# A triangular inverse done in place by columns, alpha folded into the residual addition, and new matmul prices for the list schedule

## Chip, cores and metric

The kernel runs on one core of one Trainium2 chip. The metric is device time in microseconds (us), median of several runs. The engines are named as the profile names them: PE (TensorE, matmuls; PEld is its weight loads), DVE (VectorE), ACT (ScalarE), POOL (GpSimd) and SP (SyncE, which issues the DMAs here).

## What is computed

Two transformer-like blocks of two layers each, for 256 tokens of 1024 features. The first block has modulated RMS norms, SwiGLU feed-forward parts, a differential attention with pooling, and a short convolution. The second block has deep-norm residuals, `layer_norm(alpha * h + branch)`, around a feed-forward part, a hybrid mixer and a second feed-forward part. The hybrid mixer holds a gated delta rule, for which a unit lower triangular system is solved per head and chunk. Cut to what matters here:

```
h = layer_norm(ALPHA * h + 0.5 * swiglu(h, ...), g1, b1)      # ALPHA = 4 ** 0.25, eps 1e-5
mix = hybrid_mixer(h, ...)                                    # delta rule + convolution (31 taps) + latent attention
h = layer_norm(ALPHA * h + mix, g2, b2)
h = layer_norm(ALPHA * h + 0.5 * swiglu(h, ...), g3, b3)
# inside the delta rule, per head and chunk:
a_mat = where(strict, beta * (k @ k.T) * decay, 0) + eye      # unit lower triangular
sol = triangular_solve(a_mat, rhs)
```

## The kernel before

Activations lie as [128 features, 256 tokens] tiles. Every large product is made of three fp32r matmuls (high times high, high times low, low times high): ACT casts a weight block to its high part (`whi<-raw`), DVE subtracts to get the low part (`wlo<-raw,whi`), and PE multiplies both with the two parts of the activations (`h`, `a`, `r`). In the trace these products write tiles named `mm`; small products in full fp32 write tiles named `sm`.

The program does not issue in the order in which it is written. The class `Order` takes down every instruction with what it reads and writes; `Order.price` gives each a cost in us, and `Order.schedule` makes a list schedule out of these prices, six rounds backward and forward. So a changed price or a changed dependency can move any instruction of any engine. Engines then run their queues strictly in that order.

The delta rule works on two chunks of 128 tokens per layer, four heads side by side, in `delta`. `products(tt)` makes the tile `NQ`: per head the system's matrix (transposed, only its strictly upper part counts) and the queries' part, which POOL masks with `tri_le`. `unit_inverse` inverts the four systems of a chunk by doubling blocks, in seven levels. At each level POOL masks the part of N that joins two blocks (`invN<-NQ,constt`, 128x512), PE multiplies it with the known inverse X, DVE adds the identity while it takes the result out of PSUM (`invW<-sm,constt`, 128x512), PE multiplies with Y, ACT copies the result out (`invX`), PE transposes it and ACT copies that (`invY`). `unit_inverse` is called four times in all (two layers, two chunks), and in each layer the two calls run interleaved, with the products of the delta rule's output gate (`mm<-whi,h` and `mm<-wlo,h`, 128x512) and of the mixer's other parts between them. In the same stretch DVE runs the 31 taps of the convolution (`cv<-gluu,colt,cv`, 240 instructions in two layers).

Deep norm: the tile x[m] holds alpha times h. `normed_begin.done` adds each chunk of a branch, and `end` normalises, cuts x into high and low parts and then lets POOL multiply x by ALPHA for the next residual (`x<-x`, `tensor_scalar`). `plain_begin` does the same at the entry of the second block.

Of the kernel before, what the change touches and what calls it, by code (L numbers as in the profile page):

```python
# [33 lines left out]
def _constants():  # L34
    """constants that depend on the shapes alone, as columns of one [128, n] array"""
# [9 lines left out]
    out.append(("cnt", np.tile(np.concatenate(cnt)[None, :], (P, 1))))  # L45
    for b in range(7):
        w = 1 << b
        out.append((f"level{b}", -1.0 * ((r // (2 * w) == c // (2 * w)) & (c // w % 2 == 1) & (r // w % 2 == 0))))
# [18 lines left out]
class Feat:  # L67
    """The activations a product reads: `norm`, pairs of (high, low) parts per 128 features. `early`: products
    that were already made, of what comes before the scale per token; `fix` mends them."""
# [5 lines left out]
class Spot:  # L75
    """a tile that gets its place when the instructions are put in order"""
# [16 lines left out]
class View:  # L93
    """a part of a Spot, with the offsets of its elements and the steps that lead to it"""
# [65 lines left out]
def lag(a, b):  # L160
    """from the end of an instruction of engine a to the start of one of b that reads what it wrote"""
    if a == b and a in ("PE", "DMA"):
        return 0.0
    return HOP[a] + (START if b == "DMA" else 0.0)


class Op:
    """instructions of one engine that follow each other"""
# [11 lines left out]
class Order:  # L180
    """Takes down the instructions of the whole computation with what they read and write, and issues them in the
    order of a list schedule: an engine that is free takes, of the instructions whose operands are there, the
    one that has to be over first if the whole is to end in time."""
# [19 lines left out]
    @contextmanager  # L203
    def in_turn(self):
        """the loads of the block go in the order in which they are written down"""
        self.turn = True
        yield
        self.turn = None

    @contextmanager  # L210
    def together(self):
        """the instructions of the block stay next to each other"""
# [31 lines left out]
    def touch(self, op, v, write, keep=False):  # L244
# [4 lines left out]
        # no two engines use a bank of PSUM at the same time  # L249
# [15 lines left out]
    def price(engine, name, out, ins, args, kw):  # L265
        """microseconds that an engine is held"""
# [9 lines left out]
        if engine == "PE":  # L276
            if name == "transpose":
                return 0.109
            return max(0.107, w / 2400.0) + 0.002 if ins[0].dt == F32R else max(0.217, w / 600.0 + 0.004)
# [26 lines left out]
    def schedule(self, canon, back):  # L306
        """list schedule; `canon`, an order that needs no more places than there are, gives the priorities. With
        `back`, time runs from the end to the beginning."""
# [5 lines left out]
        soon = {e: [] for e in ("PE", "DVE", "ACT", "POOL", "DMA")}    # by the time they can start  # L314
        now = {e: [] for e in soon}                                    # by their rank
# [5 lines left out]
        # room[kind][n]: places that stay free at step n of `canon`, with what is held by then  # L321
# [78 lines left out]
class Net:  # L400
    def __init__(self, nc, ins, cols):
# [10 lines left out]
        self.levels = [take(f"level{i}") for i in range(7)]  # L412
# [5 lines left out]
    def kept(self, shape, name, dt=F32):  # L418
        """a tile for the whole run"""
# [12 lines left out]
    def t(self, shape, name, dt=F32):  # L432
        """a short-lived tile"""
# [7 lines left out]
    def slot(self, name, dt=F32, width=T):  # L441
        """a tile of 128 features x 256 tokens that stays"""
        return self.nc.spot("big", [P, width], dt, name)

    def halves(self, name, n, width=T):
        """n pairs of tiles (high, low part)"""
        return [tuple(self.slot(f"{name}{i}{j}", F32R, width) for j in range(2)) for i in range(n)]

# [11 lines left out]
    def split(self, ap, n):  # L460
        """the (high, low) parts of the n pieces of a block of weights"""
# [8 lines left out]
        # at the start, before activations fill them, the small places serve too  # L470
# [24 lines left out]
    def linear_f(self, blocks, X):  # L495
        """blocks: DRAM APs [128, kc*M] that follow each other along the input features."""
# [1345 lines left out]
```

## Time and profile before

| | |
|---|---|
| median of 3 runs | 2349.83 us (2349.74 to 2353.2) |
| span of the profiled execution | 2349.6 us |
| PE busy | 2292.8 us, 98% |
| DVE busy | 1786.8 us, 76% |
| ACT busy | 1246.4 us, 53% |
| POOL busy | 143.4 us, 6% |

No time of its own is reported for the profiled execution; its span, from the first to the last instruction, is 0.2 us under the median. Busy PE time is modelled from the starts of pipelined matmuls, so a share of 98% says that PE is the engine to watch, not that its work could not be shorter. Where PE waits is read from short stretches.

### The profile page before, as it was taken

The numbers are of one execution on the slowest core, as the hardware profiler recorded it, in microseconds if no ns is written. First come the engines' busy times: TensorE is split into PE (matmuls) and PEld (weight loads), VectorE is DVE, ScalarE is ACT, GpSimd is POOL, SyncE is SP. The second block draws the span as 40 slices with busy tenths as digits, with TensorE's granted clock in tenths as the row PEclk, the third lists the DMA queues.
The fourth block names the chain that finished last, engine by engine and source line by source line (L and its number), as shares of the span: only waits on it lengthen the run. The fifth ranks groups of instructions, "written<-read, shape, count | busy, mean of one in ns | idle before, by whom it ended". The sixth has DMA issues, their size and how long they took to land.

```text
span 2349.6 us, 47411 instructions
## 1 busy us (share of the span) xinstructions
PE 2292.8 (98%) x18846; PEld 2260.3 (96%) x18846; DVE 1786.8 (76%) x3441; ACT 1246.4 (53%) x2129; POOL 143.4 (6%) x114
## 2 busy tenths in 40 slices
PE   5999999999999999999998999999999999999997
PEld 5999899999999999999998999999999989999997
DVE  7988998787778755665799959856856899769655
ACT  4445765455445544444573746644544655656543
POOL 0000100000000000100013000100100131002000
PEclk9999999999999999999999999999999999999998
DMA  8999478778777666765550445655565431555652
GB/s 312 340 318 324 130 272 293 269 268 293 266 254 240 186 186 189 236 187 179 167 169 17 151 140 192 207 181 183 184 186 176 147 124 49 173 163 195 196 180 84
DMA packets 139905, 470.30 MB, mean 200 GB/s; under 512 B 15777, under 2 KB 20897, under 8 KB 139682
## 3 DMA queue, kind: packets, MB, share of 16 engines
q1 hardware_dynamic: 139682, 467.27, 60.9%
q8 instruction: 148, 2.42, 0.4%
q14 instruction: 75, 0.61, 0.1%
HBM read 466.15 MB, written 1.05 MB: 199 GB/s over the span
## 4 chain that ended last, share of the span: by engine, by line
PE 83%; issue 8%; DVE 6%; DMA 2%; POOL 1%; ACT 0%; SPq 0%; POOLq 0%; DVEq 0%; ACTq 0%
PE mm L397 77%; PE sm L397 6%; DVE wlo L397 1%; DVE cv L397 1%; DMA raw<-in_w_ada_dram 1%; DVE x L397 1%; DMA raw<-in_ffn_wu_dram 0%; POOL x L397 0%; DVE raw L397 0%; DVE h L397 0%; DVE invW L397 0%; DVE invY L397 0%; DVE r L397 0%; DMA raw<-in_ffn_wg_dram 0%; DVE NQ L397 0%
## 5 line engine op out<-in xcount | busy, mean ns | idle before, releaser
L397 PE MATMUL mm<-h,whi 128*128 128x256 f32 x6848 | 1231.6, 282 | 11.2 <-DVE h L397 5.9
L397 ACT CAST whi<-raw 128x1024 fp32r<-128x1024 f32 (+5 forms) x811 | 786.1, 974 | 790.0 <-PE mm L397 381.6
L397 DVE TENSOR_TENSOR wlo<-raw,whi 128x1024 fp32r<-128x1024 f32 (+5 forms) x811 | 912.3, 1131 | 344.6 <-PE mm L397 281.4
L397 PEld LDWEIGHTS mm<-h,whi 128*128 128x128 f32 x6848 | 1054.3, 189 | 13.0 <-DVE h L397 7.5
L397 PE MATMUL mm<-h,wlo 128*128 128x256 f32 x3424 | 964.2, 282 | 0.2 <-DVE wlo L397 0.2
L397 PEld LDWEIGHTS mm<-h,wlo 128*128 128x128 f32 x3424 | 647.4, 189 | 0.4 <-DVE wlo L397 0.4
L397 PE MATMUL mm<-a,whi 128*128 128x256 f32 x2816 | 500.9, 281 | 0.0
L397 PEld LDWEIGHTS mm<-a,whi 128*128 128x128 f32 x2816 | 431.7, 188 | 0.1
L397 PE MATMUL mm<-a,wlo 128*128 128x256 f32 x1408 | 395.4, 281 | 0.0
L397 PEld LDWEIGHTS mm<-a,wlo 128*128 128x128 f32 x1408 | 265.1, 188 | 0.0
L397 DVE CUSTOM_DVE_ANT_0 raw<-raw,crep 128x1024 f32<-128x1024 f32 x144 | 175.5, 1221 | 67.6 <-DMA raw<-in_w_ada_dram 66.7
L397 PE MATMUL mm<-r,whi 128*128 128x258 f32 (+1 forms) x832 | 155.1, 287 | 0.0
L397 PEld LDWEIGHTS mm<-r,whi 128*128 128x128 f32 (+1 forms) x832 | 129.7, 190 | 0.0
L397 POOL TENSOR_TENSOR rstd<-var,constt 128x2 f32<-128x2 f32 x18 | 17.4, 966 | 1773.7 <-DVE var L397 1494.0
L397 PE MATMUL mm<-r,wlo 128*128 128x258 f32 (+1 forms) x416 | 118.8, 286 | 0.1
L397 DVE SCALAR_TENSOR_TENSOR cv<-gluu,colt,cv 128x256 f32<-128x256 f32 x240 | 116.9, 533 | 0.0
L397 ACT CAST a<-av 128x256 fp32r<-128x256 f32 x176 | 67.9, 404 | 40.2 <-DVE av L397 39.3
L397 ACT ACTIVATE sg<-mm 128x256 f32<-128x256 f32 x158 | 59.9, 380 | 55.2 <-PE mm L397 51.5
L397 DVE TENSOR_TENSOR a<-av,a 128x256 fp32r<-128x256 f32 x176 | 70.4, 421 | 24.7 <-ACT a L397 24.3
L397 PEld LDWEIGHTS mm<-r,wlo 128*128 128x128 f32 (+1 forms) x416 | 79.2, 190 | 0.4 <-DVE wlo L397 0.3
L397 POOL TENSOR_SCALAR x<-x 128x256 f32<-128x256 f32 x48 | 61.9, 1313 | 212.4 <-DVE h L397 212.4
L397 DVE TENSOR_TENSOR av<-mm,sg 128x256 f32<-128x256 f32 x158 | 65.9, 419 | 6.5 <-PE mm L397 5.5
(334 smaller groups left out, 2226.9 us busy)
## 6 DMA issues: line engine op xcount, KB each, us to landing
raw<-in_w_ada_dram SPq DMA_DIRECT2D x144, 512.0 KB, 4.9
raw<-in_ffn_wg_dram SPq DMA_DIRECT2D x88, 512.0 KB, 5.0
raw<-in_ffn_wu_dram SPq DMA_DIRECT2D x88, 512.0 KB, 4.7
raw<-in_ffn_wd_dram SPq DMA_DIRECT2D x64, 512.0 KB, 4.7
raw<-in_wi_gate_dram SPq DMA_DIRECT2D x48, 512.0 KB, 3.6
raw<-in_f1g_dram SPq DMA_DIRECT2D x44, 512.0 KB, 4.3
raw<-in_f1u_dram SPq DMA_DIRECT2D x44, 512.0 KB, 4.2
raw<-in_f2g_dram SPq DMA_DIRECT2D x44, 512.0 KB, 4.4
```

The costliest lines, as they stand in the source:

```text
L397: fn(*[real(a) for a in args], **{k: real(v) for k, v in kw.items()})
```

## The change

Three things change together.

1. `unit_inverse` works in place. POOL masks N once per call (`strict`), DVE adds the identity to it, and PE's first product of each level reads that whole matrix as its stationary operand, but only the columns of X that change at this level (64 of 128 per head). The part that joins two blocks is selected when DVE takes the product out of PSUM, by a multiplication with `level{b}` (128x256). The second product has 64 columns too. At the last level only a 64x64 quarter is made. ACT copies the changed columns back into X, with a stride.
2. ALPHA is no longer multiplied into x by POOL (48 `tensor_scalar` instructions). Since a layer norm does not see a common factor, x is kept as h, the residual is `ALPHA / scale * x + branch`, and eps is divided by scale squared. Chunks 0 to 3 get their factor where the branch is added, chunks 4 to 7 where the common shift is taken off.
3. `Order.price` has other prices for matmuls.

```diff
+    out.append(("strict", r < c))
     for b in range(7):
         w = 1 << b
-        out.append((f"level{b}", -1.0 * ((r // (2 * w) == c // (2 * w)) & (c // w % 2 == 1) & (r // w % 2 == 0))))
+        join = (r == c) - 1.0 * ((r // (2 * w) == c // (2 * w)) & (r // w % 2 == 1) & (c // w % 2 == 0))
+        if b == 0:
+            out += [("pair", join), ("pair_t", join.T)]
+        else:
+            out.append((f"level{b}", join[:, i // w % 2 == 0]))
...
-            return max(0.107, w / 2400.0) + 0.002 if ins[0].dt == F32R else max(0.217, w / 600.0 + 0.004)
+            return 0.0044 + w * 0.0004445 if ins[0].dt == F32R else max(0.224, w / 600.0 + 0.006)
...
         def done(m, ps):
-            nc.vector.scalar_tensor_tensor(out=x[m], in0=ps, scalar=scale, in1=x[m], op0=ALU.mult, op1=ALU.add)
+            if m < 4:
+                nc.vector.scalar_tensor_tensor(out=x[m], in0=x[m], scalar=ALPHA / scale, in1=ps, op0=ALU.mult, op1=ALU.add)
+            else:
+                nc.vector.tensor_tensor(out=x[m], in0=x[m], in1=ps, op=ALU.add)
...
-                for k in list(range(4, KD)) + list(range(4)):
+                for k in range(4, KD):
+                    nc.vector.scalar_tensor_tensor(out=x[k], in0=x[k], scalar=ALPHA / scale, in1=pb, op0=ALU.mult,
+                                                   op1=ALU.subtract)
+                for k in range(4):
                     nc.vector.tensor_tensor(out=x[k], in0=x[k], in1=pb, op=ALU.subtract)
...
                 self.cut(norm[m], x[m])
-                nc.gpsimd.tensor_scalar(out=x[m], in0=x[m], scalar1=ALPHA, scalar2=None, op0=ALU.mult)
...
-        nc.vector.scalar_tensor_tensor(out=var, in0=mm[:, 1], scalar=1e-5, in1=var, op0=ALU.add, op1=ALU.subtract)
+        nc.vector.scalar_tensor_tensor(out=var, in0=mm[:, 1], scalar=eps, in1=var, op0=ALU.add, op1=ALU.subtract)
...
     def unit_inverse(self, Nt):
         nc = self.nc
-        wide = [P, 4, P]
-        eye = self.ident.unsqueeze(1).to_broadcast(wide)
...
+        wide, H = [P, 4, P], P // 2
+        over = lambda m: m.unsqueeze(1).to_broadcast([P, 4, m.shape[1]])
+        nc.gpsimd.tensor_tensor(out=Nt, in0=Nt, in1=over(self.strict), op=ALU.mult)
+        nc.vector.tensor_tensor(out=Nt, in0=Nt, in1=over(self.ident), op=ALU.add)
...
-        for b in range(7):
-            # minus the part of N that joins two blocks
-            m = self.t(wide, "invN")
-            nc.gpsimd.tensor_tensor(out=m, in0=Nt, in1=self.levels[b].unsqueeze(1).to_broadcast(wide), op=ALU.mult)
-            ps = four(m, X) if b else turned(m)
-            w = self.t(wide, "invW")
-            nc.vector.tensor_tensor(out=w, in0=ps, in1=eye, op=ALU.add)
-            if b == 0:
-                X, Y = w, self.t(wide, "invY")
-                nc.vector.tensor_tensor(out=Y, in0=m, in1=eye, op=ALU.add)
-            elif b < 6:
-                X = kept(four(Y, w), "invX")
-                Y = kept(turned(X), "invY")
+        X, Y = self.t(wide, "invX"), self.t(wide, "invY")
+        nc.vector.tensor_tensor(out=X, in0=turned(Nt), in1=over(self.pair), op=ALU.mult)
+        nc.vector.tensor_tensor(out=Y, in0=Nt, in1=over(self.pair_t), op=ALU.mult)
+        for b in range(1, 7):
+            n = 1 << b
+            first = lambda h: X[:, h].rearrange("p (a t n) -> p a t n", t=2, n=n)[:, :, 0]
+            ps = self.psumx([P, 4, H])
+            for h in range(4):
+                nc.tensor.matmul(ps[:, h].rearrange("p (a n) -> p a n", n=n), Nt[:, h], first(h), start=True, stop=True)
+            w = self.t([P, 4, H], "invW")
+            nc.vector.tensor_tensor(out=w, in0=ps, in1=over(self.levels[b]), op=ALU.mult)
+            ps = self.psumx([P, 4, H])
+            if b < 6:
+                for h in range(4):
+                    nc.tensor.matmul(ps[:, h], Y[:, h], w[:, h], start=True, stop=True)
+                nc.scalar.copy(out=X.rearrange("p h (a t n) -> p h a t n", t=2, n=n)[:, :, :, 0],
+                               in_=ps.rearrange("p h (a n) -> p h a n", n=n))
+                ps, Y = turned(X), self.t(wide, "invY")
+                nc.scalar.copy(out=Y, in_=ps)
             else:
-                Y = kept(four(w, Y), "invY")
+                for h in range(4):
+                    nc.tensor.matmul(ps[0:H, h], w[:, h], Y[:, h, H:], start=True, stop=True)
+                nc.scalar.copy(out=Y[0:H, :, H:], in_=ps[0:H])
         return Y
```

What the schedule makes of it, at three places. First POOL's queue in the delta rule of the first hybrid layer, from the queries' and keys' norms (`rqk`) on. Before:

```order
L397 TENSOR_TENSOR rqk<-rqk,constt 128x16
L397 TENSOR_TENSOR invN<-NQ,constt 128x512 x12
L397 TENSOR_TENSOR rstd<-var,constt 128x2
L397 TENSOR_TENSOR invN<-NQ,constt 128x512 x2
L397 TENSOR_TENSOR NQ<-NQ,constt 128x512 x2
L397 TENSOR_TENSOR rstd<-var,constt 128x2
L397 TENSOR_TENSOR ro<-sso,constt 128x4 x2
```

Of the change, at the same place:

```order
L403 TENSOR_TENSOR rqk<-rqk,constt 128x16
L403 TENSOR_TENSOR NQ<-NQ,constt 128x512 x3
L403 TENSOR_TENSOR rstd<-var,constt 128x2
L403 TENSOR_TENSOR NQ<-NQ,constt 128x512
L403 TENSOR_TENSOR rstd<-var,constt 128x2
L403 TENSOR_TENSOR ro<-sso,constt 128x4 x2
```

Fourteen level masks and two `tri_le` masks of NQ became four 128x512 instructions: the strict mask and the `tri_le` mask of each chunk.

DVE's queue in the same stretch. Before, from the low part of a weight block (`wlo`) over the second chunk's first Y to two additions of the identity (`invW`), of which the second stands behind five taps of the convolution (`cv`):

```order
L397 TENSOR_TENSOR wlo<-raw,whi 128x1024
L397 TENSOR_TENSOR invY<-invN,constt 128x512
L397 TENSOR_TENSOR invW<-sm,constt 128x512
L397 TENSOR_TENSOR kfac<-rqk,eg 128x4
L397 TENSOR_SCALAR var<-sm 128x2
L397 SCALAR_TENSOR_TENSOR cv_15992<-gluu,colt,cv_15992 128x256
L397 SCALAR_TENSOR_TENSOR cv_16036<-gluu,colt,cv_16036 128x256
L397 SCALAR_TENSOR_TENSOR cv_15992<-gluu,colt,cv_15992 128x256
L397 SCALAR_TENSOR_TENSOR cv_16036<-gluu,colt,cv_16036 128x256
L397 SCALAR_TENSOR_TENSOR cv_15992<-gluu,colt,cv_15992 128x256
L397 TENSOR_TENSOR invW<-sm,constt 128x512
```

Of the change, at the entry of the first chunk's inverse: the addition of the identity to NQ (`NQ<-NQ,constt`), the first Y and the first X:

```order
L403 SCALAR_TENSOR_TENSOR NQ<-sm,rqk,decay 128x2x128
L403 SCALAR_TENSOR_TENSOR gluu<-glus,glua 128x256
L403 TENSOR_TENSOR sq<-sq 128x256
L403 SCALAR_TENSOR_TENSOR cv_15858<-gluu,colt,cv_15858 128x256
L403 TENSOR_TENSOR sq<-sq 128x256
L403 SCALAR_TENSOR_TENSOR NQ<-sm,rqk,decay 128x2x128
L403 TENSOR_TENSOR NQ<-NQ,constt 128x512
L403 SCALAR_TENSOR_TENSOR NQ<-sm,rqk,decay 128x2x128
L403 TENSOR_TENSOR invY<-NQ,constt 128x512
L403 SCALAR_TENSOR_TENSOR NQ<-sm,rqk,decay 128x2x128
L403 TENSOR_TENSOR invX<-sm,constt 128x512
L403 SCALAR_TENSOR_TENSOR NQ<-sm,rqk,decay 128x2x128
```

The wide additions of the identity out of PSUM gave way to one addition in SBUF ahead of the first transposes; `invY` and `invX` follow with one instruction of the other chunk between them.

Second, PE's queue in the same stretch. Before, from products of X with masked N to the products `invW,invY` and `invW,invN` of the two chunks:

```order
L397 MATMUL sm<-invX,invN 128x128 x3
L397 MATMUL sm<-constt,invX 128x128 x2
L397 MATMUL sm<-invX,invN 128x128
L397 MATMUL mm<-whi,h_15227 128x512
L397 MATMUL mm<-wlo,h_15227 128x512
L397 MATMUL mm<-whi,h_15277 128x512
L397 MATMUL mm<-whi,h_15239 128x512
L397 MATMUL mm<-wlo,h_15239 128x512
L397 MATMUL mm<-whi,h_15283 128x512
L397 MATMUL sm<-invW,invY 128x128 x4
L397 MATMUL sm<-invW,invN 128x128 x4
```

Of the change, from the transposes of the first chunk's N to the first product that reads X:

```order
L403 MATMUL sm<-constt,NQ 128x128 x4
L403 MATMUL mm<-h_15236,whi 128x256
L403 MATMUL mm<-h_15294,whi 128x256
L403 MATMUL mm<-h_15236,wlo 128x256
L403 MATMUL mm<-h_15296,whi 128x256
L403 MATMUL mm<-h_15317,whi 128x256
L403 MATMUL mm<-h_15296,wlo 128x256
L403 MATMUL mm<-h_15312,whi 128x256
L403 MATMUL mm<-h_15332,whi 128x256
L403 MATMUL mm<-h_15312,wlo 128x256
L403 MATMUL sm<-constt,sq 128x1 x2
L403 MATMUL sm<-invX,NQ 128x64 x4
```

The products of the first hybrid layer that stand between two steps of the inverse are other ones, and the new products have 64 columns (128x64).

Third, SP's queue near the start of the program, where the first modulation rows (`in_w_ada`) and the first weights are loaded. Before:

```order
L397 DMA raw<-in_w_ada_dram 128x1024 x2
L397 DMA raw<-in_ffn_wg_dram 128x1024
L397 DMA raw<-in_w_ada_dram 128x1024 x2
L397 DMA raw<-in_ffn_wu_dram 128x1024
L397 DMA raw<-in_w_ada_dram 128x1024 x2
L397 DMA raw<-in_ffn_wg_dram 128x1024
```

Of the change:

```order
L403 DMA raw<-in_w_ada_dram 128x1024 x2
L403 DMA raw<-in_ffn_wg_dram 128x1024
L403 DMA poolw<-in_pool_w_dram 128x256 x2
L403 DMA raw<-in_w_ada_dram 128x1024 x2
L403 DMA raw<-in_ffn_wu_dram 128x1024
L403 DMA raw<-in_w_ada_dram 128x1024 x2
```

The two loads of the pooling weights (`poolw`, read only by the attention part of the first layer) moved from there to the first loads.

## Rows read from the trace of the kernel before

**Rows 1.** Window: length, busy us (instructions) of PE PEld DVE ACT POOL, PEclk, DMA share, GB/s.

```profile
1200.00:1300.00 100.00, 93.52 (x732) 89.52 (x731) 94.94 (x215) 52.08 (x100) 25.48 (x19) 0.97 0.25 81
```

**Rows 2.** Short windows in the delta rule of both hybrid layers, same columns.

```profile
1240.00:1250.00 10.00, 9.21 (x81) 9.05 (x80) 9.39 (x17) 1.70 (x4) 5.62 (x4) 1.00 0.09 21
1250.00:1257.00 7.00, 6.56 (x51) 6.04 (x50) 7.00 (x8) 1.94 (x6) 5.78 (x5) 1.00 0.02 3
1257.00:1263.00 6.00, 1.55 (x7) 0.96 (x7) 6.00 (x11) 1.62 (x5) 3.61 (x3) 0.88 0.10 30
1263.00:1268.00 5.00, 5.00 (x20) 4.70 (x21) 3.83 (x9) 0.59 (x1) 2.98 (x3) 0.50 0.00 0
...
1917.00:1921.00 4.00, 0.66 (x6) 0.48 (x4) 4.00 (x6) 2.73 (x5) 4.00 (x4) 0.91 0.00 0
1921.00:1931.00 10.00, 9.73 (x73) 9.43 (x74) 10.00 (x22) 3.23 (x6) 2.93 (x3) 0.86 0.08 21
1936.00:1941.00 5.00, 1.28 (x11) 1.10 (x9) 5.00 (x8) 0.00 (x0) 2.67 (x3) 0.98 0.00 0
1941.00:1948.00 7.00, 6.72 (x45) 6.54 (x45) 6.15 (x10) 2.05 (x4) 4.18 (x3) 0.77 0.10 30
```

**Rows 3.** Timeline of PE: start, us, instruction, count, [idle before, releaser].

```profile
1262.83 2.05 PE L397 MATMUL sm<-invW,invY 128*128 128x128 f32 x8 [4.45 <-DVE invW L397]
...
1980.99 1.06 PE L397 MATMUL sm<-S,dn 128*128 128x128 f32 x8
```

**Rows 4.** Timeline of DVE in the same wait, same columns.

```profile
1258.35 3.74 DVE L397 SCALAR_TENSOR_TENSOR cv<-gluu,colt,cv 128x256 f32<-128x256 f32 x5
```

**Rows 5.** DVE's groups, 1244 to 1274: busy us, mean ns, idle before.

```profile
L397 DVE SCALAR_TENSOR_TENSOR cv<-gluu,colt,cv 128x256 f32<-128x256 f32 x24 | 16.7, 750 | 0.0
L397 DVE TENSOR_TENSOR invW<-sm,constt 128x512 f32<-128x512 f32 x6 | 4.1, 681 | 1.4 <-PE sm L397 1.4
L397 DVE TENSOR_TENSOR wlo<-raw,whi 128x1024 fp32r<-128x1024 f32 x2 | 3.3, 1662 | 0.0
L397 DVE TENSOR_TENSOR invY<-invN,constt 128x512 f32<-128x512 f32 x2 | 3.1, 1574 | 0.2 <-POOL invN L397 0.2
```

**Rows 6.** DVE's groups, 1280 to 1300, and a wide one of 1176 to 1184.

```profile
L397 DVE SCALAR_TENSOR_TENSOR cv<-gluu,colt,cv 128x256 f32<-128x256 f32 x27 | 11.8, 476 | 0.0
L397 DVE TENSOR_TENSOR invW<-sm,constt 128x512 f32<-128x512 f32 x5 | 3.4, 683 | 0.1
...
L397 DVE TENSOR_TENSOR wlo<-raw,whi 128x1024 fp32r<-128x1024 f32 x2 | 2.4, 1212 | 0.0
```

**Rows 7.** POOL's groups: of 1244 to 1274 the first two, of the span the third.

```profile
L397 POOL TENSOR_TENSOR invN<-NQ,constt 128x512 f32<-128x512 f32 x14 | 18.6, 1352 | 36.3 <-DVE NQ L397 29.7 <-PE sm L397 6.6
L397 POOL TENSOR_TENSOR NQ<-NQ,constt 128x512 f32<-128x512 f32 x2 | 2.5, 1270 | 0.0
...
L397 POOL TENSOR_SCALAR x<-x 128x256 f32<-128x256 f32 x48 | 61.9, 1313 | 212.4 <-DVE h L397 212.4
```

**Rows 8.** PE timeline of a one-column product; weight loads of 72 and 128 columns.

```profile
2335.11 0.58 PE L397 MATMUL sm<-constt,s 128*128 128x1 f32 x4 [1.07 <-DVE s L397]
2335.55 0.58 PE L397 MATMUL sm<-constt,sq 128*128 128x1 f32 x4
...
L397 PEld LDWEIGHTS mm<-r,whi 128*72 128x72 f32 x32 | 4.1, 142 | 0.0
...
L397 PEld LDWEIGHTS sm<-bv,invY 128*128 128x128 f32 x8 | 1.0, 192 | 0.0
```

**Rows 9.** A DVE group of the deep norms: ns min/median/max, first and last start.

```profile
L397 DVE TENSOR_TENSOR x<-x,lnw x48: 409/421/625, 1167.0 to 2345.8; 128x256 f32<-128x256 f32 x48
```

**Rows 10.** The start: its window, and the DMA issues of poolw (KB each, us).

```profile
0.00:52.00 52.00, 28.26 (x157) 24.40 (x157) 39.56 (x98) 21.40 (x40) 0.89 (x5) 0.97 0.86 304
...
poolw<-in_pool_w_dram SPq DMA_DIRECT2D x2, 128.0 KB, 4.4
```

**Rows 11.** Who waited, 640 to 692: us in total, times, longest.

```profile
PEld sm L397 <- DVE sq L397: 4.1, 1, 4.1
```

More of the change, by code (lines that the diff above doesn't have):

```diff
@@ L411, in __init__ @@
         self.neg_mask, self.mhalf, self.inv_cnt = take("neg"), take("mhalf"), take("cnt")
-        self.levels = [take(f"level{i}") for i in range(7)]
+        self.strict, self.pair, self.pair_t = take("strict"), take("pair"), take("pair_t")
+        self.levels = [None] + [take(f"level{i}") for i in range(1, 7)]
         self.swap, self.dup, self.dup_swap = take("swap"), take("dup"), take("dupswap")
@@ L1090, in end @@
             rn = self.t([P, 2, T], "rn")
-            nc.scalar.copy(out=rn, in_=self.spread2(*self.moments(st["s1"], st["s2"], D)))
+            nc.scalar.copy(out=rn, in_=self.spread2(*self.moments(st["s1"], st["s2"], D, 1e-5 / scale ** 2)))
             norm = [] if last else self.halves("h", KD)
@@ L1115, in normed_begin, with moments @@
         return done, end
-    def moments(self, s1, s2, n):
+    def moments(self, s1, s2, n, eps):
         nc = self.nc
@@ L1139, in take @@
             self.cut(pairs[m], xm)
-            self.nc.gpsimd.tensor_scalar(out=x[m], in0=xm, scalar1=ALPHA, scalar2=None, op0=ALU.mult)
         return take, lambda x, first: Feat(pairs)
@@ L1405, in unit_inverse @@
         nc = self.nc
-        wide = [P, 4, P]
-        eye = self.ident.unsqueeze(1).to_broadcast(wide)
-        X = Y = None
-        def four(lhs, rhs):
-            ps = self.psumx(wide)
-            for h in range(4):
-                nc.tensor.matmul(ps[:, h], lhs[:, h], rhs[:, h], start=True, stop=True)
-            return ps
-        def kept(ps, name):
-            o = self.t(wide, name)
-            nc.scalar.copy(out=o, in_=ps)
-            return o
+        wide, H = [P, 4, P], P // 2
+        over = lambda m: m.unsqueeze(1).to_broadcast([P, 4, m.shape[1]])
+        nc.gpsimd.tensor_tensor(out=Nt, in0=Nt, in1=over(self.strict), op=ALU.mult)
+        nc.vector.tensor_tensor(out=Nt, in0=Nt, in1=over(self.ident), op=ALU.add)
         def turned(a):
```

## The prediction

> **What bounds the kernel now.** I read the windows first, then the timelines of PE and DVE in the longest hole, then DVE's groups with and without POOL beside them. In the 100 us from 1200, where the first inverse runs, PE is busy 93.52 us, DVE 94.94 and POOL 25.48 [rows 1]: PE, which sets the end elsewhere, has holes there, and DVE is as full as PE. The short windows show where the holes are and what they cost [rows 2]. The idle PE time is 0.79 us (1240 to 1250), 0.44 (1250 to 1257) and 4.45 (1257 to 1263); in the second hybrid layer 3.34 (1917 to 1921), 0.27 (1921 to 1931), 3.72 (1936 to 1941) and 0.28 (1941 to 1948). That is 13.3 us. The reader should also look at the clock behind a hole: after the 4.45 us the granted clock is 0.50, that is 1.2 instead of 2.4 GHz, through the whole window 1263 to 1268, although PE is busy in all 5 us; eight fp32 matmuls take 2.05 us there against 1.06 us at full clock [rows 3]. A window of length L at mean clock c loses (1 - c) L: 2.5 us there, 1.4 in 1921 to 1931 (0.86) and 1.6 in 1941 to 1948 (0.77). So the inverse's holes cost 13.3 + 5.5 = **18.8 us**, 8.2 in the first hybrid layer and 10.6 in the second.
>
> Who makes the holes? The longest ends with DVE's `invW` [rows 3], and in front of it DVE ran five taps of the convolution in 3.74 us, 0.75 us each [rows 4]. Now compare DVE with itself. From 1244 to 1274, where POOL masks, a tap takes 750 ns, a wide `wlo` 1662, `invY` 1574 [rows 5]. From 1280 on, with POOL nearly still, a tap takes 476; a `wlo` outside takes 1212 [rows 6]. Yet `invW`, which reads PSUM and only one operand from SBUF, takes 681 and 683. So DVE instructions with two SBUF operands are slowed while POOL works. The excess is 24 x 0.274 + 2 x 0.45 + 2 x 0.89 (`invY` against the equally wide `invW`) = 9.3 us in the first layer, beside 14 + 2 wide POOL masks [rows 7]: 0.58 us of DVE delay for each mask, and the sum is about what PE loses there (8.2). Queues are strict, so a late tap makes `invW` late, and PE's next product.
>
> **The change part by part.**
>
> *POOL masks.* The order shows that 16 wide POOL instructions per layer become 4. At 0.58 us each, DVE is delayed by 2.3 us per layer instead of 9.3. If PE's loss keeps its proportion to the masks, a quarter of 18.8 stays, 4.7, and **14.1 us** go. Bounds: 0, if the taps in front of `invW` are what counts, whatever their speed; and 18.8, if DVE's slack now covers all. I take the proportion, since excess and loss agree so well.
>
> The Trainium skill (SBUF — State Buffer, "Who interferes with whom") says that a DVE instruction with two SBUF inputs contends with a GpSimd instruction that reads SBUF, and that the loser blocks for the whole instruction. The trace agrees on who is slowed. By a full block of 1.27 us for each of 4 masks, 5.1 of the 9.3 us of delay would stay per layer, 10.3 of the 18.8 us with them, and the time would come out near 2340 us instead.
>
> *DVE's own part of the inverse.* Per call seven `invW` and one `invY` become two SBUF instructions of that width, one X and six of half that width from PSUM. Eight whole widths become six, a gain of DVE time of at most 2 x 0.68 = 1.4 us per call, but for PE only slack. I count 0 beyond the proportion above.
>
> *PE's work.* Products and transposes are as many as before, but 128x64. What does half the columns save? A product with one column [rows 8] comes every 0.44 / 4 = 0.11 us (start 2335.11 to 2335.55, four records), the same as a record with 128 columns (eight in 1.06 us, less the last one's tail, 0.11 [rows 3]). So the weight load of 128 columns sets the pace, and 44 of a call's 48 fp32 products save nothing. Only the four last products have a stationary operand of 64 columns. A load of 72 columns takes 142 ns against 192 for 128 [rows 8], 0.89 ns per column: 64 fewer save 57 ns on each of 8 records, 0.46 us per call, **1.8 us** for four calls. Bounds 0 and 1.8; I take 1.8. Nothing hides it, PE being full around it; if PE waits there, it is worth 0.
>
> *The entry of a call* gets longer: strict mask, addition of the identity on DVE, transposes, then `invY` and `invX` before the first product. That is one DVE instruction more in front of the transposes, 0.68 us undisturbed and 1.57 with POOL beside it. What covers it: between the last product of a chunk and the transposes of its N the order of the first layer has 30 instructions of PE (18 of weights, 12 fp32 products of two records each), at 0.11 us or more a record over 4.6 us; between the transposes and the first product that reads X stand nine `mm` and two `sq` products (four records), some 1.5 us, for `invX` with one `invY` and two `NQ` in front. This cover is thin by up to a microsecond; I count it in the 4.7 that stays.
>
> *Alpha.* POOL loses 48 multiplications, 61.9 us of its time [rows 7], which nobody waits for: x is read again only when the next branch ends. Their price is again on DVE, where `x<-x,lnw` goes from 421 to 625 ns at most [rows 9], and the norms' ends have a few short PE waits. I take **1 us**, bounds 0 and 2. On DVE the instructions are exchanged one for one and cost the same.
>
> *The start.* The order moves two loads of 128 KB in front of modulation rows [rows 10]. The core loads at 304 GB/s there, and PE is busy only 28.26 of 52 us because it waits for data. 256 KB at 304 GB/s are **0.9 us later**; bound 0, if it falls where PE has work.
>
> *New prices* change ties all over the program. PE has no holes in the long feed-forward parts, so nothing is to gain there; the one other hole is 4.1 us before 690, where DVE is late behind a `w_ada` load [rows 11]. The order around it looks the same. I count 0, with 4 us either way.
>
> Sum against the span of 2349.6: -14.1 - 1.8 - 1.0 + 0.9 = -16.0, so 2333.6, and 0.2 more for the median of the runs shown: **2334 us**.
>
> **Rivals.**
>
> *All holes close.* Both the 18.8 and the 4.1 before 690 go: 2349.8 - 18.8 - 1.8 - 2 + 0.9 - 4.1 = 2324. For it: DVE gets about 7 us per layer back. Against: DVE stays above 90% full there [rows 1].
>
> *The holes stay.* The scheduler fills DVE with taps up to what it thinks PE needs, so `invW` again arrives just late, and only 1.8 us and 1 us less 0.9 remain: 2348, no measurable change (I call within 0.2%, 4.7 us, the same). For it: 27 taps fill DVE also from 1280 on [rows 6]. Against: there, undisturbed taps leave no hole.
>
> *Slower: the longer entry.* If at each of the four entries the identity and `invY` both run beside POOL's second mask (1.57 each [rows 5]) with a disturbed `wlo` (1.66) in front, PE comes 4.8 us late four times, 19.2 us, and each such hole costs half as much again at half clock (2.5 after 4.45 [rows 2]): 10.8. From 2334 that is 2364. It turns the sign when more than 3.9 us in all are lost per call, and reads as slower from some 5. Against it: the rows of PE between.
>
> *Columns count.* If a product's price followed its columns, 44 x 2 records in each of four calls would save 0.056 us: 19.7 us, 2314. The Trainium skill (TensorE: Matmul & The Clock Gate, "Back-to-back issue gap") has such a formula, N / 2.4 plus 2.5 ns, beside a warning that weight loads also set the spacing. The one-column rows speak against it.
>
> **How the numbers follow.** Chances: the forecast 0.60, all holes close 0.14, the holes stay 0.14, longer entry 0.06, columns 0.03, and 0.03 for a longer wait before 690 (2338). Faster by over 0.2%: 0.60 + 0.14 + 0.03 + 0.03 = 0.80; same 0.14; slower 0.06. The forecast's own range is 2326 to 2341 (a hole loss between 0 and 12). From 2322 to 2348 the range takes in the closing of all holes and most of the case that they stay; columns, the longer entry and a part of the same are left out.
>
> **What would show it.** POOL's busy time falls from 143 to below 60 us. Taps of the convolution stay near 476 ns between the masks. In the two stretches of the inverse PE's idle time is a few us in place of 13.3, and no window has a clock of 0.50. Records of products with 64 columns still start 0.11 us apart; the last level's start closer. A wait of PE for `invX` or the first `invW` would show the longer entry. The forecast fails if a hole that is no matter of POOL opens elsewhere, above all at the `w_ada` loads, or if the clock falls again behind one wait that is left.

## The result, and the profile after

The changed kernel takes 2368.43 us (median of 4 runs, 2364.04 to 2371.42); the kernel before, run beside it, 2349.78. The ratio is 1.0079 (95% interval 1.0066 to 1.0092): **slower by 18.7 us**, where a gain of 16 us was forecast. The profiled execution took 2366.18 us, its span is 2364.4. Its engines (busy us, share of the span, instructions):

```profile
PE 2302.6 (97%) x18846; PEld 2263.2 (96%) x18846; DVE 1756.5 (74%) x3445; ACT 1243.5 (53%) x2134; POOL 53.7 (2%) x42
```

POOL went from 143.4 to 53.7 us as forecast. But PE, with the same number of products, is busy longer and holds a smaller share of the span. The windows show where. First the two stretches of the inverse, which answer to [rows 1], and the start, which answers to [rows 10]:

```profile
1200.00:1300.00 100.00, 97.17 (x799) 93.94 (x797) 97.83 (x244) 61.89 (x129) 9.53 (x6) 1.00 0.35 111
1900.00:2000.00 100.00, 98.44 (x791) 94.91 (x792) 97.38 (x234) 54.36 (x105) 12.61 (x7) 0.98 0.29 95
0.00:52.00 52.00, 30.29 (x166) 25.91 (x166) 40.99 (x99) 20.72 (x39) 0.91 (x5) 1.00 0.89 309
```

and the second stretch before:

```profile
1900.00:2000.00 100.00, 92.38 (x715) 88.31 (x714) 97.81 (x209) 51.34 (x122) 26.15 (x20) 0.97 0.20 64
```

I count a window's loss as its idle PE time and (1 - clock) times its length. At 1200 and 1900 PE was busy 93.52 us [rows 1] and 92.38, both at clock 0.97: a loss of 6.5 + 7.6 + 3.0 + 3.0 = 20.1 us. Now it is 2.8 + 1.6 + 2.0 = 6.4. The changed kernel reaches its inverses later, at 1281 and 1956 us, and runs them past the ends of these windows; PE loses nothing from 1300 to 1360 and from 2000 to 2050. So the forecast's gain is there: 13.7 us. The loss lies in the first block, where none of the changed instructions stand. The changed kernel there:

```profile
150.00:175.00 25.00, 19.00 (x143) 17.79 (x142) 18.51 (x40) 9.35 (x15) 0.00 (x0) 0.91 0.80 272
175.00:200.00 25.00, 25.00 (x205) 25.00 (x204) 19.91 (x32) 10.15 (x13) 0.00 (x0) 0.95 0.92 318
225.00:250.00 25.00, 20.18 (x133) 18.75 (x133) 18.24 (x44) 13.07 (x19) 0.70 (x1) 0.80 0.73 249
500.00:525.00 25.00, 20.76 (x158) 19.31 (x156) 20.77 (x44) 11.15 (x17) 0.00 (x0) 0.94 0.81 256
525.00:550.00 25.00, 25.00 (x196) 25.00 (x196) 22.26 (x45) 12.33 (x20) 0.70 (x1) 0.92 0.70 233
700.00:725.00 25.00, 20.33 (x149) 19.55 (x149) 20.05 (x47) 13.43 (x19) 1.52 (x1) 0.86 0.82 287
```

and the kernel before at two of these places, and at its one hole, 675:

```profile
150.00:175.00 25.00, 25.00 (x214) 25.00 (x213) 20.98 (x40) 13.11 (x21) 0.00 (x0) 1.00 0.89 301
225.00:250.00 25.00, 25.00 (x151) 22.19 (x151) 22.38 (x56) 17.24 (x27) 2.67 (x3) 1.00 0.59 199
...
675.00:700.00 25.00, 21.11 (x156) 20.82 (x155) 18.58 (x48) 14.21 (x22) 1.54 (x1) 0.86 0.73 248
```

These six windows and the one from 300 to 350, with 1.4 us idle, lose 8.25 + 1.25 + 9.8 + 1.4 + 5.75 + 2.0 + 8.2 = 36.6 us, 15.5 of it by the clock (0.80 in 225 to 250). Before, only 675 to 700 loses: 3.9 idle + 3.5 by the clock, 7.4. The change's last window, 700 to 725, holds that same hole, come later by what was lost ahead of it: in both kernels PE waits there for DVE's `sq` (3.9 us before, 4.5 now). So the first block loses **29.2 us** more; less the 13.7 of the inverse and 3.6 of the first 52 us, 12 of the 14.8 us between the two spans are found, the rest in pieces of a us or two.

What does PE wait for there? The chain of work that ended last, in 50 to 260, with its shares by line; before:

```profile
by line: PE mm L397 97.9%; DMA raw<-in_ffn_wu_dram 2.5%; PE sm L397 1.1%; ACT whi L397 0.5%; DVE h L397 0.2%; ACT h L397 0.2%; issue 0.0%
```

and of the change:

```profile
by line: DMA raw<-in_w_ada_dram 36.9%; PE mm L403 30.4%; issue 11.2%; DVE wlo L403 10.2%; DMA raw<-in_ffn_wg_dram 3.6%; DVE raw L403 1.7%; ACT whi L403 1.2%; DVE r L403 1.2%; DVE adas L403 0.7%; DVE a L403 0.6%; PE sm L403 0.5%; DVE x L403 
```

Before, PE follows itself. Now loads of `w_ada` are more than a third of the chain. Who waited in 50 to 250 (us in total, times, longest), of the change:

```profile
DVE raw L403 <- DMA raw<-in_w_ada_dram: 29.6, 26, 3.0
...
SPq L403 <- DVE adas L403: 64.5, 34, 4.2
SPq L403 <- DVE wlo L403: 57.7, 50, 5.6
```

and before:

```profile
DVE raw L397 <- DMA raw<-in_w_ada_dram: 1.1, 1, 1.1
...
SPq L397 <- DVE wlo L397: 100.6, 62, 4.5
...
SPq L397 <- DVE adas L397: 17.3, 18, 2.0
```

`raw<-raw,crep` is DVE's reduction of a 512 KB piece of `w_ada`; its sum goes to `adas`. DVE now stands 26 times in front of a piece that has not landed, 29.6 us, against once. A piece, like a weight block, holds one of five `raw` places until DVE is through with it, and SP, whose queue is strict too, waits for a free place before it can issue a load. All its waits together are as long as before, 167.2 us against 166.3. What changed is who holds the place: it stands 64.5 us behind `w_ada` pieces (17.3 before) and 57.7 behind weight blocks that are still to be cut (100.6). So places that weights had are held by pieces that wait for DVE. I read it so that each late piece makes the next load late; the rows show the waits, not this order of cause and effect. From 100 to 150 the core loads at 298 GB/s, and before at 333, while PE, with weights cut ahead, is still full in both, first the change and then before:

```profile
100.00:150.00 50.00, 50.00 (x426) 50.00 (x425) 39.08 (x57) 21.93 (x33) 0.00 (x0) 1.00 0.87 298
```

```profile
100.00:150.00 50.00, 50.00 (x424) 50.00 (x423) 42.78 (x64) 24.05 (x34) 0.00 (x0) 1.00 0.93 333
```

From 156 us PE waits. DVE's timeline shows the first long hole made (start, us, instruction, [idle before, releaser]):

```profile
166.91 1.22 DVE L403 CUSTOM_DVE_ANT_0 raw<-raw,crep 128x1024 f32<-128x1024 f32 x1 [3.00 <-DMA raw<-in_w_ada_dram]
...
168.06 1.22 DVE L403 TENSOR_TENSOR wlo<-raw,whi 128x1024 fp32r<-128x1024 f32 x1
```

ACT's, at the same place:

```profile
168.57 0.83 ACT L403 CAST whi<-raw 128x768 fp32r<-128x768 f32 x1 [2.48 <-DMA raw<-in_ffn_wd_dram]
```

and PE's:

```profile
166.21 0.40 PE L403 MATMUL mm<-a,whi 128*128 128x256 f32 x2
...
169.76 0.84 PE L403 MATMUL mm<-a,whi 128*128 128x256 f32 x2 [3.03 <-ACT a L403]
```

DVE waits 3.00 us for a piece of `w_ada`, and a `wlo` stands behind it, which ends at 169.3. ACT waits 2.48 us for a weight block (`ffn_wd`), and behind it in ACT's queue stands the cast of `a` that PE needs, which starts at 169.3 too. PE idles 3.03 us, and its next two products take 0.84 us instead of 0.40; the granted clock is 0.66 from 170 to 180. Both strands begin with a load that comes late, and they end too close together to tell which of them held PE.

### The profile page after: what moved, and what is told of

Its sections match the earlier page's. It is cut to its first block, busy times and chain, and to the rows that moved or that the text cites. A ratio compares the mean times of both kernels' runs of the same rounds, so it can differ in the third digit from the quotient of the medians.

```text
span 2364.4 us, 47327 instructions
## 1 busy us (share of the span) xinstructions
PE 2302.6 (97%) x18846; PEld 2263.2 (96%) x18846; DVE 1756.5 (74%) x3445; ACT 1243.5 (53%) x2134; POOL 53.7 (2%) x42
## 4 chain that ended last, share of the span: by engine, by line
PE 80%; DVE 9%; DMA 7%; issue 2%; ACT 1%; POOL 0%; SPq 0%; DVEq 0%; POOLq 0%; ACTq 0%
PE mm L403 74%; PE sm L403 6%; DMA raw<-in_w_ada_dram 5%; DVE wlo L403 3%; DVE cv L403 1%; DVE raw L403 1%; DMA raw<-in_ffn_wg_dram 1%; DVE x L403 1%; DVE r L403 1%; DVE sq L403 0%; DVE h L403 0%; ACT whi L403 0%; DVE NQ L403 0%; DVE dnc L403 0%; DMA raw<-in_w_in_c_dram 0%
## 5 line engine op out<-in xcount | busy, mean ns | idle before, releaser
L403 PE MATMUL mm<-r,whi 128*128 128x258 f32 (+1 forms) x832 | 163.0, 294 | 9.2 <-ACT r L403 6.9
L403 DVE SCALAR_TENSOR_TENSOR cv<-gluu,colt,cv 128x256 f32<-128x256 f32 x240 | 106.4, 499 | 0.6
L403 ACT ACTIVATE sg<-mm 128x256 f32<-128x256 f32 x158 | 59.8, 378 | 29.2 <-PE mm L403 24.0
L403 PE MATMUL mm<-whi,h 128*128 128x512 f32 x160 | 58.5, 412 | 0.0
```

Of the source, the lines that this page charges most:

```text
L403: fn(*[real(a) for a in args], **{k: real(v) for k, v in kw.items()})
```

## Experiments

Times are medians; ratios are to the kernel before, run beside each. Its medians were 2349.35 (first four), 2348.35 (next four) and 2348.17 (last three).

**E1, old prices.**

```diff
-            return 0.0044 + w * 0.0004445 if ins[0].dt == F32R else max(0.224, w / 600.0 + 0.006)
+            return max(0.107, w / 2400.0) + 0.002 if ins[0].dt == F32R else max(0.217, w / 600.0 + 0.004)
```

> The changed kernel with the matmul prices of the kernel before, so only the inverse and alpha are changed. Theory P (the new prices reorder the first block so that DVE waits for w_ada loads, which cost PE some 31 us up to 725): the holes of 150 to 725 are gone and the time is about 2334 us, the forecast. Theory I (the inverse or alpha reorder the first block by themselves, for instance through the early poolw loads, and the prices are innocent): about 2366 us with the same holes. Theory L (the list schedule answers every small change with another order, some with holes and some without, and no part is to blame by itself): anything between, with holes at other places.

2331.45 us (four runs from 2327.22 to 2337.71), ratio 0.9933 (0.9911 to 0.9955). Theory P. The places of the holes are full:

```profile
150.00:175.00 25.00, 25.00 (x213) 25.00 (x213) 22.33 (x39) 13.28 (x21) 0.00 (x0) 1.00 0.91 331
225.00:250.00 25.00, 25.00 (x146) 21.98 (x146) 23.25 (x59) 16.32 (x26) 3.89 (x3) 1.00 0.56 178
1200.00:1300.00 100.00, 98.86 (x804) 95.08 (x804) 96.74 (x253) 58.28 (x138) 11.44 (x9) 1.00 0.28 86
1900.00:2000.00 100.00, 98.08 (x747) 90.06 (x746) 96.49 (x250) 63.38 (x160) 8.70 (x8) 1.00 0.26 81
```

The inverse's stretches lose 3.1 us here, 17.0 less than before.

**E2, new prices alone.** The kernel before with the `+` line of the change's price.

> The kernel before with only the new matmul prices. Theory P: slower by some 25 to 31 us, 2375 to 2381 us, with DVE waiting for w_ada loads between 150 and 725. Theory I: 2350 us, no change. Theory L: no fixed sign, some holes at places of its own.

2395.08 us, ratio 1.0198 (1.0183 to 1.0214): 45.7 us slower, the same holes in the first block (DVE's wait for `w_ada` in 50 to 250 is 30.4 us, 25 times). Theory P, some 14 us above its range. In windows of 10 us the stretch from 60 to 730 loses 39.2 us against 7.4 before, so the first block gives the 31 that were expected. The rest is spread over the second block: some 2 us in the old inverse, 5 from 1200 to 1220 and other small pieces.

**E3, the inverse alone**, and **E4, alpha alone**, each put into the kernel before with its old prices, by its part of the change's diff.

> The kernel before with only the inverse in place (old prices, alpha multiplied by POOL as before). Theory P: 2335 us, 14 to 16 us faster, and no holes in the first block. Theory I with the inverse to blame: about 2367 us. Theory L: the inverse's own gain of 14 to 18 us, read between 1200 and 2000, plus or minus holes elsewhere.

> The kernel before with only alpha folded into the residual addition (old prices, old inverse). Theory P: 2349 us, 1 us faster and nothing that a few rounds can tell from no change. Theory I with alpha to blame: some 2380 us with the holes of 150 to 725. Theory L: holes at places of its own, although alpha touches only the second block.

E3: 2333.35 us, ratio 0.9933 (0.9918 to 0.9947), 16.0 us faster. E4: 2348.07 us, ratio 0.9995 (0.9986 to 1.0004), not to be told from no change. Theory P in both. E4 shows one thing more. Up to 725 us every queue of it has the instructions of the kernel before in the same order, and yet its trace loses 2.9 us from 60 to 730, where the kernel before loses 7.4, all at the hole before 690. So the size of that hole in one trace is partly chance. In E1 and E3 the `poolw` loads stand where they stood before, at 216 and 217 us, so neither the inverse nor alpha moves them.

**Why do the prices do this?** While the first feed-forward runs, the program asks for 0.8 pieces of `w_ada` per weight block, that is for 1.8 loads; after the attention part of the first layer it asks for 0.5 (`ADA_RATES = 0.8, 0.0, 0.5`). A block feeds 24 products. So four more kernels each change how one of these, the product or the load, is priced.

**E5**, of the change:

```diff
-            return 0.0044 + w * 0.0004445 if ins[0].dt == F32R else max(0.224, w / 600.0 + 0.006)
+            return max(0.107, w / 2400.0) + 0.002 if ins[0].dt == F32R else max(0.224, w / 600.0 + 0.006)
```

> The changed kernel with the old price for fp32r products and the new one for fp32 products. In the first feed-forward of the first block 24 fp32r products and 1.8 loads belong together: with the old price the schedule reckons 24 x 0.109 = 2.62 us of PE against 1.8 x 1.454 = 2.62 us of loads, with the new one 24 x 0.1182 = 2.84 against 2.62. Theory R (the fp32r price alone tips that balance, so that loads and w_ada reductions no longer count as urgent, and the load stream falls behind): about 2331 us, as with all old prices. Theory F (the fp32 price matters too): clearly over 2340.

2331.52 us, ratio 0.9929 (0.9912 to 0.9945). The new fp32 price does no harm; the fp32r price is the one that does.

**E6, a longer latency of loads**, of the change with its new prices:

```diff
-HOP = {"PE": 0.31, "DVE": 0.13, "ACT": 0.14, "POOL": 0.1, "DMA": 1.0}
+HOP = {"PE": 0.31, "DVE": 0.13, "ACT": 0.14, "POOL": 0.1, "DMA": 2.05}
```

> The changed kernel, new matmul prices, with 2.05 instead of 1.0 us from the end of a load's price to its use, so that issue to use is 4.7 us in the schedule as in the trace (before it reckons 1.2 + 1.454 + 1.0 = 3.65). Theory D (what is too short in the schedule's eyes is the latency of a load: DVE's w_ada reductions are placed a microsecond before their data land): most of the 31 us come back, some 2335 to 2345. Theory R (the ratio of load price to PE price counts, not the latency): still holes in the first block, 2355 to 2370.

**E7, a dearer load**, of the change with its new prices:

```diff
-            return n(v) * v.shape[0] / 128 * 0.00142
+            return n(v) * v.shape[0] / 128 * 0.00154
```

> The changed kernel, new matmul prices, with the price of a load raised by 8.5% from 1.454 to 1.577 us per 512 KB (the rate the trace shows in that stretch, 334 GB/s, gives 1.57). 1.8 loads then cost 2.84 us in the schedule, as much as the 24 products. Theory R: the holes of the first block are gone, 2330 to 2338 us. Theory D: little changes, 2355 to 2370. Theory L (any new order is a draw): no fixed place.

E6: 2337.12 us, ratio 0.995 (0.9935 to 0.9966). E7: 2346.61 us, ratio 0.9988 (0.9978 to 0.9998). Each theory has a part, in a stretch of its own. The two traces come from runs of nearly the same time, 2342.65 us (the slowest of E6's four) and 2341.88 (the fastest of E7's ten). Windows of E6:

```profile
225.00:250.00 25.00, 18.83 (x104) 17.26 (x105) 20.01 (x44) 13.53 (x23) 0.70 (x1) 0.86 0.63 203
500.00:525.00 25.00, 23.27 (x193) 22.86 (x192) 22.80 (x43) 12.88 (x20) 1.61 (x1) 1.00 0.66 220
675.00:700.00 25.00, 24.40 (x205) 24.12 (x204) 21.03 (x48) 13.06 (x18) 0.70 (x1) 1.00 0.85 299
```

and of E7:

```profile
225.00:250.00 25.00, 24.72 (x144) 21.84 (x145) 21.75 (x53) 18.38 (x28) 3.13 (x3) 1.00 0.74 234
500.00:525.00 25.00, 21.75 (x162) 21.45 (x163) 22.17 (x41) 11.10 (x18) 0.69 (x1) 0.86 0.70 220
675.00:700.00 25.00, 20.44 (x161) 19.29 (x161) 20.54 (x44) 13.18 (x20) 0.00 (x0) 0.98 0.79 265
```

E7 leaves 0.3 us idle in 225 to 250, 1.9 in 200 to 225 and none in 150 to 175, where 1.8 loads stand beside 24 products, but keeps the holes at 500 and 675, where a block has 1.5 loads. E6 leaves 1.7 and 0.6 us idle there, and keeps 6.2 at 225. Theory R, which took the price for all, is too narrow.

**E8, the old ratio broken from the other side**: all old matmul prices, and `0.00131` in the line of E7.

> The changed kernel with all old matmul prices, and the price of a load lowered by 8% to 1.341 us per 512 KB: 1.8 loads cost 2.41 us against 2.62 of PE, the ratio of the changed kernel, although no matmul price is new. Theory R: the holes come back at the same places, some 2355 to 2370 us, with SP waiting for w_ada reductions between 50 and 150. Rival (the new matmul prices do it in another way, for instance through PE's own order): about 2331 us.

2360.58 us, ratio 1.0034 (1.0014 to 1.0053): 29 us slower than E1 by the medians (19 to 30 over its five runs), with the old matmul prices.

```profile
150.00:175.00 25.00, 21.97 (x172) 21.57 (x172) 19.69 (x40) 10.06 (x16) 0.00 (x0) 0.94 0.84 285
225.00:250.00 25.00, 20.65 (x142) 19.59 (x142) 20.61 (x50) 15.65 (x24) 0.70 (x1) 0.86 0.65 216
700.00:725.00 25.00, 21.09 (x152) 20.67 (x151) 22.44 (x58) 12.55 (x21) 1.54 (x1) 0.86 0.56 175
```

The holes of the changed kernel are back at its places (the one at 500 too, with 3.3 us idle), and Theory R's range is met. So a load priced too low against PE opens them without any new matmul price, and it is no draw of the order. The ratio is not all of it: E7, which restores it, keeps some of the holes, and E6, which leaves it as in the change, is rid of some.

**E9, both corrections of the load**, the edits of E6 and E7, with the new matmul prices.

> The changed kernel, new matmul prices, with both corrections of the loads together: 1.577 us per 512 KB and 2.05 us from its end to the use. The price alone cleared the first 175 us but left holes at 475 to 550 and 675 to 725, where a block has 1.5 loads and the schedule still sees slack; the latency alone cleared those and left some 9 us at 200 to 250. Theory RD (both are needed, each for its stretch, and the matmul prices are harmless once the loads are priced as truly): first block without holes, 2326 to 2333 us. Theory L (each order is a draw): 2335 to 2360, holes at new places.

2328.9 us, ratio 0.9919 (0.9902 to 0.9935). Its windows:

```profile
225.00:250.00 25.00, 24.36 (x150) 21.64 (x149) 22.53 (x51) 16.79 (x26) 3.56 (x2) 1.00 0.64 224
...
675.00:700.00 25.00, 25.00 (x213) 25.00 (x213) 22.73 (x57) 15.88 (x26) 1.54 (x1) 1.00 0.63 212
```

Theory RD. The new matmul prices do no harm once the loads are priced by what the trace shows. Side by side, with the loss from 60 to 730 (my sum over windows of 10 us) and the time that DVE waited for `w_ada`, all in us:

| kernel | fp32r price | load price | load latency | loss, 60 to 730 | waits, 50 to 250 | waits, 450 to 725 |
|---|---|---|---|---|---|---|
| before | old | old | old | 7.4 | 1.1 | 41.8 |
| E1 | old | old | old | 1.0 | 0.5 | 22.2 |
| the change | new | old | old | 36.4 | 29.6 | 54.2 |
| E7 | new | dearer | old | 19.5 | 5.3 | 50.2 |
| E6 | new | old | longer | 13.2 | 15.3 | 16.6 |
| E9 | new | dearer | longer | 1.6 | none | 11.8 |
| E8 | old | cheaper | old | 25.0 | 11.3 | 47.3 |

The waits of the first stretch go mostly with the price, those of the second with the latency. A wait of DVE alone does not make a hole: the kernel before has 41.8 us of it in the second stretch and loses 7.4.

**E10, POOL's masks given back**, on E1, in each level of the inverse:

```diff
+            idle = nc.gpsimd.tensor_tensor(out=self.t(wide, "invM"), in0=Nt, in1=over(self.strict), op=ALU.mult)
             w = self.t([P, 4, H], "invW")
...
+                op.before.add(idle)
```

> The changed kernel with old matmul prices (2331.45 us), and twelve 128x512 multiplications per hybrid layer given back to POOL in the inverse, whose results nobody reads: six per call, one a level, as before. DVE's, ACT's and PE's own work is that of the changed kernel. Theory C (the forecast's: POOL's masks slow DVE's two-operand instructions by 0.58 us each, and PE loses as much): 7 us per layer come back, some 2343 to 2347 us, with convolution taps at 700 ns and more in the inverse. Theory W (the holes closed because DVE's and PE's own work in the inverse got less or moved; POOL beside it hardly matters to PE): 2330 to 2335 us.

2352.56 us, ratio 1.0014 (1.0004 to 1.0024): 21.1 us more than E1 by the medians. Windows of E10:

```profile
1200.00:1300.00 100.00, 93.51 (x737) 88.75 (x736) 97.41 (x230) 51.47 (x111) 23.89 (x19) 0.97 0.22 66
1900.00:2000.00 100.00, 91.94 (x702) 86.60 (x701) 94.74 (x213) 48.66 (x122) 25.36 (x20) 0.93 0.19 60
```

DVE's taps of the convolution in 1235 to 1275 (busy us, mean ns), of E10:

```profile
L403 DVE SCALAR_TENSOR_TENSOR cv<-gluu,colt,cv 128x256 f32<-128x256 f32 x44 | 26.3, 648 | 0.0
```

and of E1:

```profile
L403 DVE SCALAR_TENSOR_TENSOR cv<-gluu,colt,cv 128x256 f32<-128x256 f32 x54 | 25.0, 510 | 0.0
```

Theory C, and more than it asked: 6.5 + 8.1 us idle and 3.0 + 7.0 by the clock, 24.6, against 3.1 in E1. DVE's, ACT's and PE's own work is the same, and no engine waits for one of the new masks in the trace, so what they cost comes of standing beside DVE, or of the order that they leave, which differs from E1's from 336 us on.

**E11, old matmul prices with E6's latency.**

> The changed kernel with old matmul prices and the truer latency of loads (2.05 us for 1.0). Its first block has no holes with old prices, so the latency can gain only 2 us around 690; 2326 to 2333 us if order elsewhere stays as good. Theory L: several us either way.

2326.46 us, ratio 0.9911 (0.9896 to 0.9926): the fastest here, 21.7 us under the kernel before. DVE's wait for `w_ada` in 450 to 725 falls from 22.2 us in E1 to 2.9. Its interval overlaps those of E1 and E9, so the last few us are not certain. It comes near the 2324 of the rival in which all holes close.

## Why the prediction was wrong

**The step that failed** is the one on the new prices: "PE has no holes in the long feed-forward parts, so nothing is to gain there ... I count 0, with 4 us either way." That there is nothing to gain does not mean that there is nothing to lose. Measured: 37.0 us by the medians (the change against E1), or 45.7 on the old inverse (E2). The full windows of PE were a balance. In 100 to 150 the kernel before makes 424 products, 24 in 2.83 us, and loads at 333 GB/s with the DMA engines 0.93 busy: 512 KB in 1.57 us, 1.8 of them in 2.83. PE and the loads are both nearly full. The old prices had both 8% too cheap (2.62 and 2.62), and so in balance. The new price corrected one side only: by its prices the schedule now has 8% of slack for the loads. That this opens the holes is shown (E1, E5, E8); that the schedule ranks loads and reductions as less urgent for it is my reading of the program, and no run shows the ranks. The prediction's last lines did name the place, a hole "above all at the `w_ada` loads", but as a thing to look for: it had 0.03 and 4 us, with no price worked out for a whole stretch that falls behind. The latency adds to it. The schedule reckons 1.2 + 1.454 + 1.0 = 3.65 us from issue to use; the page of the changed kernel (KB each, median us from issue to landing) says

```profile
raw<-in_w_ada_dram SPq DMA_DIRECT2D x144, 512.0 KB, 4.7
```

about a microsecond more; E6 and E9, which put it in, show that it matters. That the order "looks the same" around the `w_ada` hole was read off the sequence; how far ahead the loads run was not considered. That hole before 690 [rows 11] may be the same fault, already in the kernel before: E9's trace does not have it (25.00 busy in 675 to 700). But since E4 has less than half of it with the very same order, one trace without it is weak evidence.

Two smaller slips in the prediction's numbers: five taps in 3.74 us [rows 4] are not 0.75 us each: two, beside masks, take 1.32 and 1.31, and three take 0.47; and a hole loss of 0 gives 2329, not the 2326 at which its own range starts.

**The inverse's holes** (forecast -14.1): -13.7 in the changed kernel, -17.0 in E1. E3's 16.0 us stand beside the forecast's -14.1 - 1.8 = -15.9 (E3 has no early `poolw` loads), and that they agree so closely is partly luck: in E3's trace the inverse's stretches give 17.0, the hole before 690 another 5.7, and some 5 are lost anew between 1300 and 1900. E10 speaks for POOL's masks as the cause: given back, they bring the loss back. In the stretch where a tap took 750 ns [rows 5], the change has (1260 to 1310):

```profile
L403 DVE SCALAR_TENSOR_TENSOR cv<-gluu,colt,cv 128x256 f32<-128x256 f32 x69 | 30.3, 498 | 0.0
```

But the 0.58 us per mask was only DVE's part. E10's 24 masks cost the kernel 21.1 us, 0.88 each: 11.5 us of idle PE time and 10.0 by the clock in the two windows.

**The longer entry** is real, and small. The largest piece, with POOL's, DVE's and PE's rows:

```profile
1276.30 2.78 POOL L403 TENSOR_TENSOR NQ<-NQ,constt 128x512 f32<-128x512 f32 x2 [30.37 <-DVE NQ L403]
...
1276.80 1.33 DVE L403 SCALAR_TENSOR_TENSOR cv<-gluu,colt,cv 128x256 f32<-128x256 f32 x1
1278.05 1.32 DVE L403 TENSOR_TENSOR sq<-sq 128x256 f32<-128x256 f32 x1
...
1279.68 0.68 DVE L403 TENSOR_TENSOR NQ<-NQ,constt 128x512 f32<-128x512 f32 x1
...
1280.51 0.63 PE L403 MATMUL sm<-constt,NQ 128*128 128x128 f32 x4 [1.50 <-DVE NQ L403]
```

A tap takes 1.33 and a square 1.32 us beside two POOL masks (2.78 us), against 0.48 and 0.43 for the same instructions just ahead; the identity comes late, and PE waits 1.50 us. That rival had 4.8 per call.

These rows also show what a mask does to DVE. Taken one by one, the first mask runs from 1276.30 to 1277.84 and the second from 1277.80 to 1279.08. The tap starts 0.5 us into the first and ends 0.3 us after it; the square starts 0.25 us into the second and ends 0.3 us after it. Each waited for about what was left of its mask and then did its work. The Trainium skill (SBUF — State Buffer, "Who interferes with whom") calls the port pair that DVE shares with GpSimd an exclusive lock. The trace agrees: the tap lost 0.85 us where 1.04 of its mask were left, the square 0.89 where 1.03 were left. So the prediction's 0.58 us per mask is a mean over instructions that came early in a mask, late in it, or not at all, and its full block for every mask was too much.

**The small terms.** Products with 64 moving columns cost what those with 128 did, as forecast, and the last level's are closer:

```profile
1990.75 0.68 PE L403 MATMUL sm<-invY,invW 128*64 128x64 f32 x8
1991.36 1.10 PE L403 MATMUL sm<-invW,invY 128*128 128x64 f32 x8
1992.27 0.48 PE L403 MATMUL mm<-whi,h 128*128 128x512 f32 x1
```

Eight records with 128 stationary columns take 0.91 us (1991.36 to 1992.27), eight with 64 take 0.61 (from 1990.75): 0.30 saved per call and 1.2 in all, not 1.8. Alpha: 1 us forecast, 1.3 by the medians of E4, within its uncertainty of none. The early `poolw` loads: no 0.9 us to be seen; PE is busy 30.29 of the first 52 us against 28.26 [rows 10], and E9 and E11, which have them early too, are the two fastest kernels here.

**What stays open.** E7 and the old prices have the same ratio of 1.5 loads to 24 products (0.83), yet E7 loses 19.5 us in the first block and E1 1.0; the kernel before, with old prices, has one of E7's holes, the one before 690. That the truer latency cures them is shown (E9); why cheap PE prices hide them is not. A guess from the prices alone: they bring every deadline 8% nearer than it is.

## What to carry to other kernels

Prices that steer an order work in good part as ratios. Before correcting one of them, look in the trace for the stretches where two resources are both nearly full (here PE, and the DMA engines at 0.93), and ask which of them the order will think idle afterwards; then correct the other one and the latency with it (E9). The latency could here be corrected by itself (E11). A window in which the bounding engine is full says nothing about how little keeps it so: look at what is ahead of it (loads in flight, places that are free, strict queues behind a wait).

## What was not expected of the hardware

A hole costs PE more than its idle time, and more than the prediction's half as much again: in E10, 14.6 us idle in two windows of 100 us came with another 10.0 by the granted clock (0.97 and 0.93). And POOL beside DVE cost the kernel more than the 0.58 us a mask by which the forecast saw it delay DVE: 24 results that nobody reads, on an engine that is busy about 3% of the span, slowed it by 21 us.
